# A state-space layer's chunk recurrence as a real scan after a rotation, with a new order of the stage

## The chip, the cores and the metric

The kernel runs on one core of a Trainium2 chip. The metric is the device time of one execution in microseconds (us); three runs of the kernel before gave 2777.58, 2775.36 and 2776.45 us, so a median of 2776.45.

## The reference

The model is two transformer blocks over 512 positions of width 1024. The first has two layers of a token mixer and a feed-forward part (ffn1). The second has a layer with an S5 state-space mixer and a layer with stick-breaking attention, each followed by a feed-forward part with a convolution. The change touches the S5 mixer only:

```python
u = (h @ w_in).astype(f32).reshape(bsz, seq, N_GROUPS, SSM_GROUP)
dt = jnp.exp(log_dt.astype(f32))[:, None]
mag = jnp.exp(a_re * dt)
ab_re = mag * jnp.cos(a_im * dt)
ab_im = mag * jnp.sin(a_im * dt)
...
bu_re = jnp.einsum('blgh,gph->blgp', u, bb_re)
bu_im = jnp.einsum('blgh,gph->blgp', u, bb_im)
# s[t] = ab * s[t-1] + bu[t], in complex numbers, over the sequence
_, _, s_re, s_im = lax.associative_scan(
    combine, (a_seq_re, a_seq_im, bu_re, bu_im), axis=1)
y = (jnp.einsum('blgp,ghp->blgh', s_re, c_re.astype(f32))
     - jnp.einsum('blgp,ghp->blgh', s_im, c_im.astype(f32))
     + d_skip.astype(f32) * u)
y = jax.nn.gelu(y.reshape(bsz, seq, D_SSM)).astype(h.dtype)
z = y @ w_glu
return z[..., :D_MODEL] * jax.nn.sigmoid(z[..., D_MODEL:])
```

There are 64 groups of 16 channels, and each group has 64 complex states.

## The kernel before

The sequence is cut into 64 chunks of 8 positions. Inside a chunk the work is done by matmuls with tables that are made beforehand; from chunk to chunk runs a recurrence with the factor ab to the power of 8. The channels are done in 8 tiles of 8 groups. In a tile of states one half of the 128 partitions holds the real parts and the other the imaginary parts, for 8 groups x 64 chunks. For tile i the stage has these steps, by the names that the order uses:

- `u` (four pieces, 24 matmuls): the projection w_in. VectorE takes it out of PSUM in another order of elements (`ev_u`, L1390), ScalarE's queue writes it to DRAM (`ud`), SyncE's queue reads it back with positions on the partitions (`U`).
- `S` (`states`, 8 matmuls of 64 columns, tile `vps`): what each chunk adds to the state. ScalarE copies it into `VS` (L1404).
- `c` (`scan`): the recurrence over 64 chunks, on VectorE, for parts of 2, 3 and 3 tiles: seven steps inside blocks of 8 chunks, seven from block to block, each of five operations (L1427 to L1431), a turn on ScalarE (`hs`, L1446), and for each tile three operations that make the correction `fx` (L1453 to L1455).
- `T` (`lags`, tile `yps<-U,tt`): the part of the output that comes from inside the chunk. `O` (`outs`): the part from the states, 8 matmuls on `VS` and 8 on `fx`, into the same PSUM tile.
- `G`, `H`: the gelu, Square and tanh on ScalarE and two operations on VectorE (`gq`, L1479, L1480, L1486), then a write to DRAM on ScalarE's queue (`yd`) and a read on SyncE's queue (`yT`) that turns the layout back.
- `Y` (`ysplit`): `yT` is cut into a high and a low part, `yhl`, the high one on ScalarE (L1494) and the low one on VectorE (L1495).
- `g`: tile k's share of the first four outputs of w_glu, 12 matmuls of 512 columns that read `yhl` and the split weights. The remaining w_glu outputs follow as ordinary work.

`w`, `x` and `o` load a tile's tables `wt`, `tt`, `ot` (512 KB each). A weight comes as `raw` and is split into `wh` (ScalarE, L230) and `wl` (VectorE, L233); a split is planned by a running count of TensorE's work and waits for a buffer that an earlier weight's matmuls release. The order of the stage is written out by hand in the table `ORDER`; every engine runs its instructions strictly in program order, and an instruction that issues a DMA on ScalarE's or SyncE's queue waits there as well. All tiles of 128x512 take their storage from one set of 16 slots, so a new tile waits for the last reader of the tile that had its slot.

The tables of the state-space stage are made in `ssm_gen`, as background work between the matmuls of ffn1 of the first block's second layer, from 1183 to 1425 us: `mag`, `angle`, `factor`, then `inner` and `outer` (powers of ab by doubling, `powers`, L1231 to L1237), and for each of the 8 tiles the matrices behind `ot`, `tt` and `wt`, with `go` and `gw` as tiles on VectorE and `gps` as their products on TensorE. `outer` writes `SR` and `SI`, which the scan reads.

Of the kernel before, what the change touches and what calls it, by code (L numbers as in the profile page):

```python
# [53 lines left out]
for _name, _w in (("ident", 128), ("ones_d", 128), ("ones_q", 128), ("ones_kv", 128), ("blk", 128),  # L54
# [2003 lines left out]
```

## Time and profile before

| what | before |
|---|---|
| median of three runs | 2776.45 us |
| profiled execution: its time | 2783.61 us |
| its span | 2781.9 us |
| mean granted clock of TensorE | 0.983 |
| TensorE busy | 2714.6 us (98% of the span) |
| VectorE busy | 1844.2 us (66%) |
| ScalarE busy | 1302.5 us (47%) |
| state-space stage from S0 on | 1555.33 to 1691.1 us |

TensorE is busy nearly everywhere. A busy matmul is not one at full speed: in the slices the granted clock stands at 9 tenths or more but for two slices, about 1590 to 1690 us, with 8 and 6 tenths. They are the state-space stage. "Idle before" an instruction is the time in which its engine did nothing, and the name behind the arrow is what came last before it could start.

### The profile page before, as it was taken

To read this page: it belongs to the slowest core of one execution; us is meant where nothing else is said; L and a number is where in the kernel's file an instruction comes from. 1 tells how busy PE (TensorE), PEld (TensorE's weight loads), DVE (VectorE), ACT (ScalarE), POOL (GpSimd) and SP (SyncE) were. 2 spreads that over 40 slices of the span, in tenths; PEclk is the share of its full clock that TensorE was granted. 3 is DMA by queue.
4 is the path that set the end of the run, shared out by engine and by line. 5 is a ranking of instruction groups with operands and counts; after the bars stand their busy time and mean duration, and the time that the engine had idled before them with its cause. 6 is when DMAs were issued, how large, how long until landed. Compare 5 with 4: busy or idle time off the path is not lost.

```text
span 2781.9 us, 35330 instructions
## 1 busy us (share of the span) xinstructions
PE 2714.6 (98%) x13470; PEld 2277.4 (82%) x13470; DVE 1844.2 (66%) x2963; ACT 1302.5 (47%) x2204; POOL 292.8 (11%) x311
## 2 busy tenths in 40 slices
PE   8999999999999999999999889999999999999998
PEld 6888888888878888888888788888887888888887
DVE  7889863444687997787745784555456777574544
ACT  6567553332466664533334213433235888542323
POOL 1000020000210100221002000010111111110111
PEclk9999999999999999999999868999999999999999
DMA  5323333333232334354434623333324323233321
GB/s 206 116 77 90 124 117 97 98 99 99 91 110 90 93 95 158 114 188 148 144 123 174 186 87 99 97 100 95 95 87 136 88 84 114 84 99 99 99 91 61
DMA packets 122650, 309.56 MB, mean 111 GB/s; under 512 B 35824, under 2 KB 42736, under 8 KB 122352
## 3 DMA queue, kind: packets, MB, share of 16 engines
q1 hardware_dynamic: 109424, 291.57, 32.5%
q0 software_dynamic: 2432, 7.34, 1.2%
q10 hardware_dynamic: 10624, 8.39, 1.0%
q8 instruction: 106, 1.74, 0.3%
q14 instruction: 64, 0.52, 0.1%
HBM read 260.59 MB, written 41.68 MB: 109 GB/s over the span
## 4 chain that ended last, share of the span: by engine, by line
PE 52%; DVE 5%; ACT 5%; issue 2%; POOL 1%; DMA 0%; SPq 0%; DVEq 0%; POOLq 0%; ACTq 0%
PE mm L312 46%; PE yps L312 2%; DVE wl L233 1%; PE s L312 1%; ACT e L1674 1%; PE o L312 1%; ACT e L1673 1%; ACT e L1678 1%; PE vps L312 1%; ACT wh L230 1%; DVE xg L360 0%; ACT sp L356 0%; ACT whl L356 0%; ACT w L1694 0%; PE gps L312 0%
## 5 line engine op out<-in xcount | busy, mean ns | idle before, releaser
L312 PE MATMUL mm<-xg,wh 128*128 128x512 f32 (+1 forms) x4080 | 1224.0, 382 | 26.5 <-DVE xg L360 15.7
L312 PEld LDWEIGHTS mm<-xg,wh 128*128 128x128 f32 x4080 | 747.3, 188 | 182.7 <-DVE xg L360 24.6
L230 ACT ACTIVATE wh<-raw 128x1024 fp32r<-128x1024 f32 (+2 forms) x417 | 431.0, 1039 | 826.8 <-PE mm L312 524.4
L312 PE MATMUL mm<-xg,wl 128*128 128x512 f32 (+1 forms) x2024 | 759.9, 378 | 0.0
L233 DVE TENSOR_TENSOR wl<-raw,wh 128x1024 fp32r<-128x1024 f32 (+2 forms) x417 | 528.0, 1270 | 164.7 <-ACT wh L230 159.6
L312 PE MATMUL mm<-hid,wh 128*128 128x512 f32 (+1 forms) x1816 | 539.0, 380 | 0.7 <-DVE hid L357 0.5
L312 PEld LDWEIGHTS mm<-xg,wl 128*128 128x128 f32 x2024 | 381.8, 189 | 71.3 <-issue 0.2
L312 PEld LDWEIGHTS mm<-hid,wh 128*128 128x128 f32 x1816 | 335.0, 188 | 66.8 <-DVE hid L357 1.4
L312 PE MATMUL mm<-hid,wl 128*128 128x512 f32 (+1 forms) x908 | 344.0, 379 | 0.0
L312 PE MATMUL mm<-yhl,wh 128*128 128x512 f32 x640 | 210.2, 408 | 6.9 <-DVE yhl L1495 3.7
L414 POOL TENSOR_TENSOR acc<-acc,sq 128x256 f32<-128x256 f32 (+1 forms) x90 | 106.7, 1185 | 963.7 <-ACT sq L402 875.8
L312 PEld LDWEIGHTS mm<-hid,wl 128*128 128x128 f32 x908 | 170.8, 188 | 31.9
L312 PEld LDWEIGHTS mm<-yhl,wh 128*128 128x128 f32 x640 | 122.2, 196 | 33.3 <-DVE yhl L1495 5.3
L1582 POOL TENSOR_TENSOR gt<-gt,cv 128x512 f32<-128x512 f32 x44 | 78.1, 1775 | 589.5 <-ACT wh L230 467.9
L312 PE MATMUL mm<-yhl,wl 128*128 128x512 f32 x320 | 128.6, 402 | 0.0
L591 DVE SCALAR_TENSOR_TENSOR ht<-mm,rr 128x512 f32<-128x512 f32 x64 | 43.8, 690 | 116.9 <-PE mm L312 116.6
L1590 DVE SCALAR_TENSOR_TENSOR xr<-mm,xr 128x512 f32<-128x512 f32 (+1 forms) x50 | 33.5, 670 | 124.5 <-PE mm L312 124.5
L607 DVE TENSOR_TENSOR part<-part,mm 128x512 f32<-128x512 f32 (+1 forms) x52 | 33.5, 645 | 113.9 <-PE mm L312 113.9
L1570 DVE SCALAR_TENSOR_TENSOR gt<-mm,rr 128x512 f32<-128x512 f32 x88 | 60.6, 690 | 68.1 <-PE mm L312 68.0
L722 DVE TENSOR_REDUCE nm<-s 128x1 f32<-128x512 f32 x128 | 86.7, 683 | 21.0 <-PE s L312 20.6
L749 ACT ACTIVATE pt<-pT 128x512 fp32r<-128x512 f32 x128 | 74.6, 593 | 46.3 <-PE pT L328 44.3
L729 ACT ACTIVATE p<-s,nm 128x512 f32<-128x512 f32 x128 | 87.0, 683 | 11.0 <-DVE nm L722 8.9
(295 smaller groups left out, 3461.2 us busy)
## 6 DMA issues: line engine op xcount, KB each, us to landing
raw<-in_w_up SPq DMA_DIRECT2D x152, 512.0 KB, 3.6
raw<-in_w_down SPq DMA_DIRECT2D x96, 512.0 KB, 3.5
raw<-in_w_in SPq DMA_DIRECT2D x51, 512.0 KB, 3.5
xd<-xr SPq DMA_DIRECT2D x16, 512.0 KB, 2.7
gd<-z SPq DMA_DIRECT2D x32, 256.0 KB, 2.1
g<-gd SPq DMA_DIRECT2D x32, 256.0 KB, 4.0
raw<-in_w_o SPq DMA_DIRECT2D x16, 512.0 KB, 3.6
raw<-in_w_glu SPq DMA_DIRECT2D x16, 512.0 KB, 4.2
```

The source lines that it names most:

```text
L230: ins = self.nc.scalar.activation(h, x, AF.Copy)
L233: ins = lo_engine.tensor_tensor(l, x, h.bitcast(F32), ALU.subtract)
L312: return self.nc.tensor.matmul(out, lhsT, rhs, **kw)
L414: eng.tensor_tensor(st["acc"][:, cols], st["acc"][:, cols], sq[:, cols], ALU.add)
L591: nc.vector.scalar_tensor_tensor(t, ps, 0.0, st["r"], op0=ALU.max, op1=ALU.mult)
L607: nc.vector.tensor_tensor(p, p, ps[:, cols], ALU.add)
L722: nc.vector.tensor_reduce(nm, ps, AX.X, ALU.max, negate=True)
L729: nc.scalar.activation(p, ps, AF.Exp, bias=nm, accum_out=sm)
L749: nc.scalar.activation(hi[:, :, q0:q0 + 128], v, AF.Copy)
L1570: v.scalar_tensor_tensor(t, ps, -0.5, st["r"], op0=ALU.mult, op1=ALU.mult)
L1582: nc.gpsimd.tensor_tensor(t, t, sg.pop(n), ALU.mult)
L1590: v.scalar_tensor_tensor(x, ps[:, cols], 0.5, x, op0=ALU.mult, op1=ALU.add)
```

## The change

The recurrence s[c] = a s[c-1] + v[c] has a complex factor a = m e^(i t). With z[c] = e^(-i t c) s[c] it becomes z[c] = m z[c-1] + e^(-i t c) v[c], which is real in its factor. The new stage does so for each tile by itself:

- `S` now ends with two ScalarE copies of 64x512 that swap the real and the imaginary half (`vx`).
- `b` (`load_tab`) loads a table of cos and sin for tile i (512 KB) on SyncE's queue, into one of four buffers.
- `R` (`scan`): GpSimd sets the first column of the mask `m` to zero, ScalarE fills the rest with the factor's size to the power of 8, VectorE turns v by two multiplies and an add, runs one scan instruction over 128x512 (`vz`), and ScalarE makes the negated copy with the halves swapped (`zx`, two instructions).
- `Z` (`turn`): two VectorE multiplies turn back; `O` has 8 matmuls on `vz` and 8 on `zx`, so as many as before.
- The tables come from `ssm_gen`: `turns` (the angle times 8 by three squarings), two `wheel`s in place of `outer`, and for each tile six VectorE operations of 128x512 (`table`), written to DRAM.
- `load_ops` is cut into `w` and `x`, and `ORDER` is written anew. Line numbers move with it: L312 of before is L309 now, L230 is L227, and L1404 has become L1447 and L1448.

The order's beginning, before and after (c: pieces of the old scan; R and Z of the new one):

```diff
-    u5.0 u5.1 S0 S1 u5.2 c0.0 w5 u5.3 c0.1 u6.0 c0.2 u6.1 c0.3 c0.4 w6 c0.5 c0.6 c0.7 u6.2 c0.8 w4 S2 c0.9 c0.10 w7
...
+    b0 b1 o0 u5.0 b2 u5.1 S0 R0 S1 u5.2 w4 Z0 R1 u5.3 S2 b3 Z1 S3 R2 w5 u6.0 u6.1 u6.2 Z2 R3 u6.3 T0 O0 o1 Z3 x4 S4 b4 u7.0 G0 u7.1
+    T1 O1 H0 o2 x5 R4 u7.2 G1 u7.3 Z4 w6 b5 T2 O2 H1 o3 S5 x6 w7 R5 G2 T3 O3 H2 Y0 g0 o4 Z5 S6 b6 G3 R6 T4 O4 H3 o5 x7 S7 b7 Z6 Y1 g1 G4 R7
...
+        def turns():
+
+            pr, pi = g["pr"], g["pi"]
+            m8 = self.m8 = self.apool.tile([128, 64], F32, name="m8")
+            v.tensor_tensor(m8, g["mag"], g["mag"], ALU.mult)
+            x, y = T("g_th", [64]), T("g_t", [64])
+            for k in range(3):
+                v.tensor_tensor(x, pr, pr, ALU.mult)
+                v.tensor_tensor(y, pi, pi, ALU.mult)
+                v.scalar_tensor_tensor(pi, pr, 2.0, pi, op0=ALU.mult, op1=ALU.mult)
+                v.tensor_tensor(pr, x, y, ALU.subtract)
...
+                for n in (1, 2, 4):
+                    powers(R, I, n)
+                for z, x in (("r", R), ("i", I)):
+                    t = g[name + z] = self.s2("wh" + z, F32, [128, 8, 64])
+                    nc.gpsimd.tensor_copy(t, x[:, 0:8])
+                    nc.gpsimd.tensor_copy(g["p" + z], x[:, 8])
...
+            H = lambda z: g["hi" + z][:, :, gs_].rearrange("p j g -> p g j").unsqueeze(3).to_broadcast(sh)
+            L = lambda z: g["lo" + z][:, :, gs_].rearrange("p k g -> p g k").unsqueeze(2).to_broadcast(sh)
...
+                    v.tensor_tensor(o, H("r"), L(a), ALU.mult)
+                    v.tensor_tensor(x, H("i"), L(b), ALU.mult)
+                    v.tensor_tensor(box["t"][:, k], box["t"][:, k], w, op)
+                    if k == 1:
+                        nc.sync.dma_start(self.Cd[i], box["t"])
...
         def states(i):
-            k = part[i]
...
-            self.pin(nc.scalar.copy(VS[k][:, 8 * (i - a):8 * (i - a) + 8], ps))
+            f = ps.rearrange("p g c -> p (g c)")
+            x = self.s2("vx")
+            self.pin(nc.scalar.activation(x[up], f[dn], AF.Copy))
+            self.pin(nc.scalar.activation(x[dn], f[up], AF.Copy))
+            vp[i] = f, x
+
+        def load_tab(i):
+            tab[i] = self.vpool.tile([128, 2, 512], F32, name="tab", tag="tab", bufs=4)
+            nc.sync.dma_start(tab[i], self.Cd[i])
...
+            f, x = vp.pop(i)
+            m = self.vpool.tile([128, 8, 64], F32, name="m", tag="m", bufs=2)
+            nc.gpsimd.memset(m[:, :, 0:1], 0.0)
+            self.pin(nc.scalar.activation(m[:, :, 1:64], self.m8[:, 8 * i:8 * i + 8].unsqueeze(2).to_broadcast([128, 8, 63]), AF.Copy))
+            t = self.s2("vt")
+            self.pin(v.tensor_tensor(t, f, tab[i][:, 0], ALU.mult))
+            self.pin(v.tensor_tensor(x, x, tab[i][:, 1], ALU.mult))
+            self.pin(v.tensor_tensor(t, t, x, ALU.add))
+            z = self.s2("vz")
+            self.pin(v.tensor_tensor_scan(z, m.rearrange("p g c -> p (g c)"), t, 0.0, ALU.mult, ALU.add))
+            y = self.s2("zx")
+            self.pin(nc.scalar.activation(y[up], z[dn], AF.Copy, scale=-1.0))
+            self.pin(nc.scalar.activation(y[dn], z[up], AF.Copy, scale=-1.0))
+            zs[i] = z, y
+
+        def turn(i):
+            z, y = zs[i]
+            c = tab.pop(i)
+            self.pin(v.tensor_tensor(z, z, c[:, 0], ALU.mult))
+            self.pin(v.tensor_tensor(y, y, c[:, 1], ALU.mult))
```

Three places show what moves on the engines. The first is ScalarE at the beginning of the stage. `ud2` to `ud4` are the DRAM writes of u2 to u4, the `wh` between them belongs to the weights of w_glu and waits for the matmuls of u5. Before:

```order
L230 ACTIVATE wh_14447<-raw_14248 128x1024
L1392 DMA ud2_105<-u_14377 128x8x64
L1404 COPY VS0_14466<-vps_14467 128x512
L1404 COPY VS0_14466<-vps_14477 128x512
L230 ACTIVATE wh_14515<-raw_14358 128x1024
L1392 DMA ud3_106<-u_14406 128x8x64
L1392 DMA ud4_107<-u_14442 128x8x64
L1404 COPY VS1_14604<-vps_14605 128x512
```

and now:

```order
L227 ACTIVATE wh_14597<-raw_14398 128x1024
L1436 DMA ud2_113<-u_14527 128x8x64
L227 ACTIVATE wh_14693<-raw_14508 128x1024
L1436 DMA ud3_114<-u_14556 128x8x64
L1436 DMA ud4_115<-u_14592 128x8x64
L1447 ACTIVATE vx_14633<-vps_14624 64x512
L1448 ACTIVATE vx_14633<-vps_14624 64x512
L1469 ACTIVATE m_14636<-m8_11419 128x8x63
```

The copies out of S0 and S1 (`VS0`) stood ahead of that `wh` and stand now behind it and behind both writes, as `vx`.

The second place is ScalarE between the gelus of tiles 0 to 3, ahead of the first `g` block. Before, where `yhl` is tile 0's `Y`:

```order
L1479 ACTIVATE gq_14857<-yps_14803 128x512
L332 ACTIVATE gq_14857<-gq_14857 128x512
L1487 DMA yd1_112<-gq_14857 128x512
L1494 ACTIVATE yhl_14888<-yT_14825 128x512
L1404 COPY VS2_14738<-vps_14944 128x512
L1404 COPY VS2_14738<-vps_14956 128x512
L1446 ACTIVATE hs_14975<-VS1_14604 64x168 x2
L1494 ACTIVATE yhl_15034<-yT_14879 128x512
```

and now, where `vx` to `zx` are tile 5's copies and scan neighbours, `gq_14990` is tile 2's gelu, and `yhl` is tile 0's `Y`:

```order
L1505 DMA yd1_120<-gq_14904 128x512
L1447 ACTIVATE vx_14971<-vps_14962 64x512
L1448 ACTIVATE vx_14971<-vps_14962 64x512
L1469 ACTIVATE m_14978<-m8_11419 128x8x63
L1477 ACTIVATE zx_14987<-vz_14985 64x512
L1478 ACTIVATE zx_14987<-vz_14985 64x512
L1497 ACTIVATE gq_14990<-yps_14931 128x512
L329 ACTIVATE gq_14990<-gq_14990 128x512
L1505 DMA yd2_121<-gq_14990 128x512
L1512 ACTIVATE yhl_15023<-yT_14880 128x512
L1447 ACTIVATE vx_15055<-vps_15046 64x512
L1448 ACTIVATE vx_15055<-vps_15046 64x512
```

`Y0` stood behind the write `yd1` and stands now behind `yd2`, tile 2's gelu and tile 5's part of the scan. In TensorE's order g0 comes right behind O3 now, and behind S6 and S7 before.

The third place is TensorE in the background work, at tile 0's first products (`gps`), which read `go`. Before:

```order
L312 MATMUL mm_11529<-hid_11135,wh_11286 128x512 x2
L312 MATMUL mm_11529<-hid_11135,wl_11287 128x512
L312 MATMUL gps_11567<-g_c0_11496,g_bs_11492 32x16
L312 MATMUL gps_11567<-go_11499,g_bs_11492 32x112
L312 MATMUL gps_11567<-g_c0_11496,g_bs_11492 32x16
L312 MATMUL gps_11567<-go_11499,g_bs_11492 32x112
```

and now:

```order
L309 MATMUL mm_11702<-xg_10581,wh_11536 128x512 x2
L309 MATMUL mm_11702<-xg_10581,wl_11537 128x512
L309 MATMUL mm_11702<-xg_10609,wh_11536 128x512 x2
L309 MATMUL gps_11637<-go_11575,g_bs_11568 32x112
L309 MATMUL gps_11637<-g_c0_11572,g_bs_11568 32x16
L309 MATMUL gps_11637<-go_11575,g_bs_11568 32x112
L309 MATMUL gps_11637<-g_c0_11572,g_bs_11568 32x16
L309 MATMUL gps_11637<-go_11575,g_bs_11568 32x112
```

The products that read `go` followed at once behind the first one and stand now 29 matmuls later; the first one, which reads `g_c` alone, is at its old place.

## Rows read from the trace of the kernel before

**Rows 1.** Windows of the stage: columns us, busy us of each engine, granted clock, DMA.
```profile
1588.70:1626.30 37.60, 37.60 (x167) 36.44 (x166) 35.30 (x91) 9.20 (x14) 0.00 (x0) 0.50 0.44 135
...
1646.80:1657.00 10.20, 6.39 (x14) 4.61 (x15) 9.65 (x26) 1.15 (x2) 0.00 (x0) 0.50 0.21 63
...
1663.80:1691.10 27.30, 27.02 (x104) 24.13 (x104) 9.72 (x17) 5.44 (x9) 0.00 (x0) 0.50 0.21 58
...
1555.33:1691.10 135.77, 122.46 (x643) 111.39 (x642) 101.82 (x266) 26.37 (x42) 0.00 (x0) 0.72 0.39 119
```

**Rows 2.** Timeline of TensorE in the stage: start, us, line, operation, idle before.
```profile
1559.04 1.97 PE L312 MATMUL vps<-U,wt 128*128 128x64 f32 x16 [1.54 <-issue]
...
1587.73 2.78 PE L312 MATMUL yps<-VS,ot 128*128 128x63 f32 x16 [3.12 <-DVE VS L1431]
...
1620.98 1.20 PE L312 MATMUL mm<-yhl,wh 128*128 128x512 f32 x2
...
1626.25 1.91 PE L312 MATMUL yps<-U,tt 128*128 128x64 f32 x16
...
1628.00 1.95 PE L312 MATMUL yps<-VS,ot 128*128 128x63 f32 x16
...
1648.07 2.07 PE L312 MATMUL mm<-yhl,wh 128*128 128x512 f32 x4 [2.84 <-ACT yhl L1494]
...
1661.97 2.01 PE L312 MATMUL yps<-VS,ot 128*128 128x63 f32 x16 [0.97 <-DVE VS L1431]
...
1668.89 3.64 PE L312 MATMUL yps<-VS,ot 128*128 128x63 f32 x16
...
1672.32 3.60 PE L312 MATMUL yps<-fx,ot 128*128 128x49 f32 x16
```

**Rows 3.** Groups of VectorE in the stage: busy us, mean ns, idle before.
```profile
L1431 DVE TENSOR_TENSOR VS<-VS,t 128x192 f32<-128x192 f32 x14 | 7.2, 517 | 0.4
...
L1390 DVE SCALAR_TENSOR_TENSOR u<-mm,rr 128x512 f32<-128x512 f32 x6 | 6.7, 1109 | 0.0
...
L1480 DVE SCALAR_TENSOR_TENSOR gq<-gq,yps 128x512 f32<-128x512 f32 x8 | 5.5, 686 | 16.8 <-ACT gq L1479 16.8
...
L1454 DVE TENSOR_TENSOR fx<-hs,SI 128x392 f32<-128x392 f32 x8 | 4.5, 560 | 0.1
```

**Rows 4.** The same groups for ScalarE in the stage.
```profile
L1494 ACT ACTIVATE yhl<-yT 128x512 fp32r<-128x512 f32 x8 | 4.8, 625 | 10.4 <-DVE gq L1486 6.9 <-DMA yT<-yd 3.5
...
L1404 ACT COPY VS<-vps 128x512 f32<-128x512 f32 x8 | 4.7, 585 | 33.0 <-PE vps L312 26.1 <-DVE u L1390 6.9
...
L230 ACT ACTIVATE wh<-raw 128x1024 fp32r<-128x1024 f32 x3 | 3.2, 1061 | 1.8 <-PE mm L312 1.8
```

**Rows 5.** DMA issues and their landing in us; the timeline about ud3.
```profile
ud<-u ACTq DMA_DIRECT2D x8, 256.0 KB, 4.6
U<-ud SPq DMA_DIRECT2D x8, 256.0 KB, 3.0
...
1561.46 0.38 SPq L1394 DMA_DIRECT2D U<-ud  x1
...
1563.40 1.06 ACT L230 ACTIVATE wh<-raw 128x1024 fp32r<-128x1024 f32 x1 [1.76 <-PE mm L312]
```

**Rows 6.** Windows of the background work, columns as in rows 1.
```profile
1200.00:1230.00 30.00, 30.00 (x158) 24.65 (x158) 29.97 (x83) 8.35 (x12) 14.70 (x12) 1.00 0.53 192
...
1230.00:1425.00 195.00, 195.00 (x1064) 160.53 (x1063) 134.75 (x223) 61.49 (x87) 15.01 (x28) 1.00 0.48 147
```

**Rows 7.** Timeline of all engines about tile 0's first matmuls.
```profile
1217.43 0.42 DVE L1231 TENSOR_TENSOR g_w<-gp 128x256 f32<-128x256 f32 x1
...
1218.99 3.83 POOL L1262 COPY SR<-gp 128x512 f32<-128x512 f32 x1 [6.49 <-DVE gp L1233]
...
1220.24 0.69 DVE L1284 TENSOR_TENSOR go<-go,cx 128x512 f32<-128x512 f32 x1
...
1220.63 0.36 PE L312 MATMUL gps<-go,g_bs 128*32 128x112 f32 x2
```

More of the change, by code (lines that the diff above doesn't have):

```diff
@@ new lines, in wheel, with f @@
+        def wheel(name):
+            def f():
+                R, I = [self.s4("gp", F32, [128, 16, 64]) for _ in range(2)]
+                v.memset(R[:, 0], 1.0)
+                v.memset(I[:, 0], 0.0)
+                v.tensor_copy(R[:, 1], g["pr"])
+                v.tensor_copy(I[:, 1], g["pi"])
+                for n in (1, 2, 4):
[4 more added lines that the diff above has]
+                    nc.gpsimd.tensor_copy(g["p" + z], x[:, 8])
+            return f
@@ new lines, in ssm_gen, with table, part, f @@
+        ops += [load, mag, angle, factor, inner, tables, turns, wheel("lo"), wheel("hi")]
+        def table(i):
+            box = {}
+            sh = [128, 8, 8, 8]
+            gs_ = slice(8 * i, 8 * i + 8)
+            H = lambda z: g["hi" + z][:, :, gs_].rearrange("p j g -> p g j").unsqueeze(3).to_broadcast(sh)
+            L = lambda z: g["lo" + z][:, :, gs_].rearrange("p k g -> p g k").unsqueeze(2).to_broadcast(sh)
+            def part(k, a, b, op):
+                def f():
+                    if k == 0:
+                        box["t"] = self.s4("gt", F32)
+                    o = box["t"][:, k].rearrange("p (g j k) -> p g j k", g=8, j=8)
+                    w = self.s2("cx")
+                    x = w.rearrange("p (g j k) -> p g j k", g=8, j=8)
+                    v.tensor_tensor(o, H("r"), L(a), ALU.mult)
[3 more added lines that the diff above has]
+                        nc.sync.dma_start(self.Cd[i], box["t"])
+                return f
+            return [part(0, "r", "i", ALU.subtract), part(1, "i", "r", ALU.add)]
@@ new lines, in scan @@
+        def scan(i):
+            f, x = vp.pop(i)
[12 more added lines that the diff above has]
+            zs[i] = z, y
@@ L1471, in outs @@
-            fx = FX.pop(i, None)
-            for g in range(8 if fx is not None else 0):
-                self.pin(self.mm(ps.rearrange("p g (b k) -> p g b k", b=8)[:, g, 1:8, 1:8], ot[i][:, g], fx[:, g],
-                                 start=False, stop=True, skip_group_check=True))
+            for x in zs.pop(i):
+                x = x.rearrange("p (g c) -> p g c", g=8)
+                for g in range(8):
+                    self.pin(self.mm(ps[:, g, 1:64], ot[i][:, g], x[:, g, 0:63], start=False, stop=True, skip_group_check=True))
@@ L1836, in build @@
             self.Td = [dt(f"td{i}", [128, 8, 128]) for i in range(8)]
+            self.Cd = [dt(f"cd{i}", [128, 2, 512]) for i in range(8)]
             self.wt, self.tt = {}, {}
```

100 lines of the change are left out of this document (20 added, 80 removed).

## The prediction

> **What bounds the kernel now.** I read the windows first, because the change touches one stage of some 136 us and one piece of background work. From 1555.33 us, where S0 starts, to 1691.1 us the windows give TensorE 122.46 us of work in 135.77, so 13.3 us idle, at a mean granted clock of 0.72 [rows 1]. [...] TensorE's busy time in them is 37.60 + 6.39 + 27.02 = 71.0 us; at the full level it would take half, so the lower level costs 35.5 us [rows 1], and the work itself is 122.46 - 35.5 = 87 us, say 88 since the pace of small matmuls does not quite double (16 records of a T block take 1.75 us from 1626.25, and of an O block 3.43 from 1668.89) [rows 2]. So 88 us of work, 13.3 of waits, 35 of lower clock.
>
> Then the timeline of TensorE, to see what it did before the clock fell and before it rose [rows 2]. It fell behind waits of 3.12 us (for VectorE's scan) and of 2.84 us (for ScalarE's yhl), and a third time in the small matmuls that follow a wait of only 0.97 us; a wait of 1.54 us between dense work did not lower it. It rose while the 12 matmuls of 512 columns of one `g` block ran (1620.98 to 1626.25 us: 5.27 us, or 0.22 us a matmul at the full level), and the 33 us of 64-column work ahead of that, from 1587.73 on, had not raised it. So the stage is paid for in waits of TensorE and in the clock that they take away. VectorE is the engine waited for: 101.82 us busy of 135.77, and 35.30 of 37.60 in the first slow stretch [rows 1].
>
> **What the change takes away.** The scan's VectorE work: 14 steps of five operations of 0.51 us on three tiles (35.5 us) and 24 operations of 0.56 us for `fx` (13.5) [rows 3], beside seven steps on two tiles and 21 short ones: over 50 us together. In its place each tile gets five 128x512 operations and one scan instruction. The nearest row for the five is gq (0.686 us) [rows 3]; back to back they pace about 0.6. No row shows a scan. Its bounds are 0.69 us (gq) and 1.11 us (the strided u, the dearest 512-column row) [rows 3]; I take 0.7, since its operands are contiguous as gq's are. [...] A tile costs VectorE 5 x 0.6 + 0.7 = 3.7 us, eight tiles 30 us. ScalarE gains: per tile two x copies, the mask m, two y copies, each no dearer than VS's 0.585 [rows 4], 8 x 2.9 = 23 us against 4.7 for VS. TensorE's matmuls are the same in number.
>
> So the waits for VectorE of 3.12 and 0.97 us go. What is late next is ScalarE's and VectorE's strict order and the transfers, place by place:
>
> 1. S1's wait of 1.54 us stays (its place is unchanged).
> 2. S2 and S3 now stand right behind u5, ahead of all of u6. S1 ends at 1560.8, 11 matmuls of 0.22 us bring S2 to 1563.2 [rows 2]. U2 is issued at 1561.46 and lands 3.0 us later [rows 5]: 1.2 us of wait. S3 would start at 1566.2. Its ud3 stands on ScalarE's queue behind a split wh, which before started at 1563.40 and waits for u5's end in the new order too; it takes 1.06 [rows 4, 5]. ud lands 4.6 us after its issue and U 3.0 after its own [rows 5], so U3 comes at 1571 to 1572: a wait of 5 to 6 us, and less if ud lands sooner than its median. I take 5. Before, u6's matmuls covered this.
> 3. Z2's y copies stand behind a wh that waits for the end of u7, and Z2 behind its wl: 1.06 for wh [rows 4], 1.1 for wl by the strided u and 0.69 [rows 3], 2.9 us, of which T2 covers 1.75: 1.2 us.
> 4. g0 stands right behind O3. On ScalarE the copy of tile 5 out of PSUM comes ahead of G2, and by the built program it must wait for O3's last matmul, because its tile takes a storage slot that zx of tile 3 gives back. Behind it in order: two copies (1.2), mult, mult, add and scan (2.6), two y copies (1.2), gq on both engines and tanh (0.6 + 0.69 + 0.63), the second gq (0.69), and then Y0, which waits for yd2's issue (0.6) [rows 3, 4]. That is 8.2 us with no latency in it; with some ten hand-overs 9 us. Of this chain nothing overlaps TensorE, which has no other work in its order: 9 us, the longest wait of the stage.
> 5. g1 stands behind S7 and waits for its copies and yhl: 1.2 + 0.63 [rows 4], so 2 us. g5 stands behind O7's gelu, four operations of 0.6 to 0.7 us and yhl [rows 3, 4], 3.3 us less the 2.7 of g4, with hand-overs 1.4 us.
>
> The waits are 1.5 + 1.2 + 5 + 1.2 + 9 + 2 + 1.4 = 21 us, against 13.3.
>
> Then the clock. Behind S3's wait, as behind those of 2.84 and 3.12 us, I expect the lower level until part of u6 has run: S3 1.7 us and about 15 of its 24 matmuls by 0.2 us, 5 us. At O2 the nearest row is the wait of 0.97 us in front of an O block, and there it fell [rows 2]; so O2, S5, T3 and O3 (10.5 us of full-clock work, 1.75 for eight matmuls) run at the lower level, 9.5 us dearer. The 9 us wait lowers it for g0, 2.4 us; g1 1 us. That makes 18 us, against 35.
>
> [...]
>
> Stage: 88 + 21 + 18 = 127 us for 135.8, a gain of about 9.
>
> **What it adds in the background.** The tables are built during ffn1 of the layer before, where TensorE is busy all the time and VectorE 29.97 of 30 us from 1200 to 1230 us, 134.75 of 195 after [rows 6]. `turns` (16 operations of 64 columns) and a second wheel (18 operations, the widest of them, of 256 columns, 0.42 us [rows 7], a third as many of each width) come ahead of tile 0's matmuls: some 2.5 + 4 us, and up to 3.8 us more where the second wheel waits for GpSimd's copy (a strided one took 3.83 [rows 7]; these are contiguous). Tile 0's go was finished at 1220.93, just as TensorE's first matmul on it was under way (1220.63) [rows 7]. The new order puts 29 matmuls of 0.22 us in between, 6.4 us: go is wanted at about 1227, and ready at 1220.9 plus 6.5 to 10.3, so at 1227.4 to 1231.2. A wait of 0 to 4 us for TensorE. Each tile's new table is four multiplies with one operand read at a stride and two adds: 6 x 0.69 = 4.1 us by gq, or 4 x 1.11 + 1.4 = 5.8 by u [rows 3]; 33 to 47 us in all, against 195 - 134.75 = 60 us that VectorE has free. The splits made three tiles ahead hide most. I take 2 us for go and 2 us for late splits and evacuations: 4 us, between 0 and 20 (below). The 512 KB tables go out and come back on SyncE's queue in time that DMA has; I cost them at nothing, the DMA engines being at a share of 0.48 there [rows 6], and where this cover is gone a late table costs what U3 does, some 4 us.
>
> Sum: the profiled run took 2783.6 us (span 2781.9, 1.7 around it). 2783.6 - 9 + 4 = 2778.6; the median of the runs shown, 2776.45, lies 7.2 below the profiled run, so 2771.4, say 2772 us for the median.
>
> **The rivals.**
> First, the clock holds through O2 and g1: surcharge 5 + 2.4 = 7.4, stage 88 + 21 + 8 = 117, gain 19, with 4 in the background: 2761 us. For it: 1.54 us did not lower the clock [rows 2]. Against it: 0.97 did.
> Second, slower: VectorE becomes the bound in the background. By the dear price it needs 47 + 10 of the 60 us that it has free, so nearly every burst of a table (5.8 us in one piece) makes a split or an evacuation late. It decides from about 1.1 us a multiply on. Eight tiles by 2 us and 4 for go are 20 us; with the stage at -9 that is 2776.5 + 11 = 2787 us. For it: VectorE at 29.97 of 30. Against it: the splits' lead and 7.5 us that VectorE has free for each tile.
> Third, the waits at S3 and g0 are shorter (3 and 5 us, G2 not held up) and the clock falls once: 88 + 15 + 6 = 109, gain 27, background 2: 2751 us.
> Fourth, the change doesn't do what it says: the lower clock stays through the 64-column work from S3 to g1 as it does today, and the stage keeps its 136 us: 2776 to 2782 us with the tables.
>
> **How the numbers follow.** A measurement of this kernel can't tell a change of less than about 0.2%, 5.6 us, from none: faster is under 2770.9, slower over 2782.0. Forecast 0.40 (own range 2764 to 2781; 0.14 of it faster, 0.22 same, 0.04 slower), first rival 0.20 (faster 0.18, same 0.02), second 0.20 (slower 0.18, same 0.02), third 0.08 (faster), fourth 0.12 (same 0.06, slower 0.06). Faster 0.40, same 0.32, slower 0.28. The range takes in the third rival's end and the second's dear one: 2750 to 2792.
>
> **What would show it.** In the new profile: TensorE idle ahead of g0 by 8 to 11 us, released by ScalarE's yhl; idle ahead of S3 by 3 to 7 us, released by U's transfer; VectorE in the stage at least 20 us below its 101.82 [rows 1]; the granted clock at 0.5 behind S3 and from O2 to g0; the scan between 0.69 and 1.11 us; TensorE idle for up to 4 us at about 1227 us, VectorE over 170 of 195 us behind it. If g0 follows O3 without a wait, or the clock stays up, the stage's sum is wrong on the dear side; if TensorE shows gaps through 1230 to 1425 us, the background's is wrong on the cheap side.

## The result and the profile after

The changed kernel took 2793.68 us (median of four runs, 2791.56 to 2795.40); the kernel before took 2775.9 us beside it. The ratio is 1.0067, with an interval of 1.0054 to 1.0079: slower by 17.8 us, where I had forecast 2772 us and no more than 2792. The profiled execution took 2794.77 us, its span is 2792.7.

The windows first, as in [rows 1, 6]: us, busy us of TensorE, its weight loads, VectorE, ScalarE and GpSimd, granted clock, DMA. The first one is the stage from S0 to the first matmul of the weights behind it.

```profile
1572.58:1706.58 134.00, 111.66 (x666) 101.32 (x665) 60.35 (x81) 44.34 (x69) 0.68 (x6) 0.80 0.44 136
...
1230.00:1425.00 195.00, 184.45 (x993) 151.56 (x994) 173.02 (x270) 58.16 (x82) 28.36 (x36) 0.96 0.51 158
```

The same cut of the stage in the trace of before:

```profile
1555.33:1696.04 140.71, 127.40 (x665) 115.45 (x664) 102.52 (x267) 27.36 (x43) 0.00 (x0) 0.73 0.38 114
```

S0 starts at 1572.58 us and not at 1555.33, so 17.25 us are lost before the stage begins, most of them in the stretch where TensorE had been busy for 195.00 of 195 us [rows 6] and is now for 184.45, at a granted clock of 0.96. The stage itself is 6.7 us shorter than in that execution, and VectorE's share of it has fallen by 42 us. In the stage, TensorE's waits are (start, us, line, operation, idle before and what ended it):

```profile
1583.21 3.65 PE L309 MATMUL vps<-U,wt 128*128 128x64 f32 x16 [3.78 <-DMA U<-ud]
1591.28 3.65 PE L309 MATMUL vps<-U,wt 128*128 128x64 f32 x16 [4.42 <-DMA U<-ud]
...
1620.19 1.89 PE L309 MATMUL yps<-U,tt 128*128 128x64 f32 x16
1623.29 2.00 PE L309 MATMUL yps<-vz,ot 128*128 128x63 f32 x16 [1.21 <-DVE vz L1484]
...
1627.72 3.62 PE L309 MATMUL vps<-U,wt 128*128 128x64 f32 x16
...
1651.46 1.52 PE L309 MATMUL mm<-yhl,wh 128*128 128x512 f32 x2 [9.88 <-ACT yhl L1512]
...
1667.88 1.52 PE L309 MATMUL mm<-yhl,wh 128*128 128x512 f32 x2 [1.94 <-ACT yhl L1512]
...
1699.16 1.43 PE L309 MATMUL mm<-yhl,wh 128*128 128x512 f32 x5 [1.00 <-ACT yhl L1512]
```

These are the waits that I had listed for S2, S3, O2, g0, g1 and g5, and they answer to [rows 2]; the 1.5 us that I had kept for S1 did not come. Behind the 1.21 us the pace goes from 1.9 us for 16 matmuls to 3.62: the clock fell there, as expected. At the beginning it fell a block sooner than I had it, at S2 (3.65 us).

In the background, TensorE waits at two places. The first is tile 0's `go`, the second the copy `g_bs` of tile 4's B matrix on GpSimd:

```profile
1229.01 0.61 PE L309 MATMUL mm<-xg,wh 128*128 128x512 f32 x2
1233.65 0.58 PE L309 MATMUL gps<-go,g_bs 128*32 128x112 f32 x2 [4.03 <-DVE go L1324]
...
1343.97 0.29 PE L309 MATMUL gps<-g_c,g_bs 128*32 128x16 f32 x2 [6.90 <-POOL g_bs L1358]
...
1346.54 1.22 PE L309 MATMUL mm<-xg,wh 128*128 128x512 f32 x2
```

The last row shows two matmuls of 512 columns in 1.22 us where they take 0.61 elsewhere: the lower clock comes on top of the wait. What made `g_bs` late stands on VectorE's timeline:

```profile
1337.11 0.69 DVE L588 SCALAR_TENSOR_TENSOR ht<-mm,rr 128x512 f32<-128x512 f32 x1 [3.35 <-PE mm L309]
1337.97 1.23 DVE L230 TENSOR_TENSOR wl<-raw,wh 128x1024 fp32r<-128x1024 f32 x1 [0.17 <-ACT wh L227]
1339.12 0.68 DVE L593 TENSOR_TENSOR hid<-hq,hid 128x512 fp32r<-128x512 f32 x1
1339.72 0.28 DVE L1346 TENSOR_TENSOR g_bb<-g_b,g_fr 128x128 f32<-128x128 f32 x1
```

VectorE had nothing to do for 3.35 us and then, in program order, took TensorE's last result (`ht`), a weight split and `hid` before it began tile 4's `g_bb`. TensorE's next instruction reads what comes of `g_bb`. So this is no lack of VectorE time: a piece of background work stands behind an evacuation that waits for TensorE, and TensorE waits for that piece. GpSimd's copy adds 2.63 us:

```profile
1340.94 2.63 POOL L1357 COPY g_bs<-g_bb 64x128 f32<-64x128 f32 x1 [17.10 <-DVE g_bb L1350]
1343.63 0.29 POOL L1358 COPY g_bs<-g_bb 64x128 f32<-64x128 f32 x1
```

### The profile page after: what moved, and what is told of

Read it like the earlier page. It is cut to its first block, busy times and chain, and to the rows that moved or that the text cites. A ratio compares the mean times of both kernels' runs of the same rounds, so it can differ in the third digit from the quotient of the medians.

```text
span 2792.7 us, 35332 instructions
## 1 busy us (share of the span) xinstructions
PE 2704.9 (97%) x13470; PEld 2267.8 (81%) x13470; DVE 1851.7 (66%) x2864; ACT 1320.8 (47%) x2230; POOL 301.1 (11%) x327
## 4 chain that ended last, share of the span: by engine, by line
PE 52%; DVE 5%; ACT 5%; issue 1%; DMA 1%; POOL 1%; SPq 0%; ACTq 0%; DVEq 0%; POOLq 0%
PE mm L309 46%; PE yps L309 2%; DVE wl L230 1%; PE o L309 1%; PE z L309 1%; PE s L309 1%; PE vps L309 1%; ACT e L1689 1%; PE gps L309 1%; ACT wh L227 1%; DVE xg L357 0%; ACT e L1693 0%; ACT e L1688 0%; ACT sp L353 0%; ACT whl L353 0%
## 5 line engine op out<-in xcount | busy, mean ns | idle before, releaser
L309 PE MATMUL mm<-xg,wh 128*128 128x512 f32 (+1 forms) x4080 | 1228.1, 384 | 26.0 <-DVE xg L357 14.7
L309 PEld LDWEIGHTS mm<-xg,wh 128*128 128x128 f32 x4080 | 750.8, 189 | 182.4 <-DVE xg L357 23.3
L227 ACT ACTIVATE wh<-raw 128x1024 fp32r<-128x1024 f32 (+2 forms) x417 | 431.1, 1039 | 851.9 <-PE mm L309 580.7
L309 PE MATMUL mm<-xg,wl 128*128 128x512 f32 (+1 forms) x2024 | 762.5, 379 | 0.0
L230 DVE TENSOR_TENSOR wl<-raw,wh 128x1024 fp32r<-128x1024 f32 (+2 forms) x417 | 532.5, 1281 | 187.0 <-ACT wh L227 179.4
L309 PE MATMUL mm<-hid,wh 128*128 128x512 f32 (+1 forms) x1816 | 539.3, 380 | 0.7 <-DVE hid L354 0.4
L309 PEld LDWEIGHTS mm<-xg,wl 128*128 128x128 f32 x2024 | 383.4, 189 | 72.5 <-issue 0.6
L309 PEld LDWEIGHTS mm<-hid,wh 128*128 128x128 f32 x1816 | 335.0, 188 | 67.0 <-DVE hid L354 1.4
L309 PE MATMUL mm<-hid,wl 128*128 128x512 f32 (+1 forms) x908 | 344.0, 379 | 0.0
L309 PE MATMUL mm<-yhl,wh 128*128 128x512 f32 x640 | 205.8, 401 | 12.8 <-ACT yhl L1512 12.8
L309 PEld LDWEIGHTS mm<-hid,wl 128*128 128x128 f32 x908 | 170.8, 188 | 32.1
L309 PEld LDWEIGHTS mm<-yhl,wh 128*128 128x128 f32 x640 | 119.7, 191 | 37.7 <-ACT yhl L1512 13.6
L309 PE MATMUL mm<-yhl,wl 128*128 128x512 f32 x320 | 127.0, 397 | 0.0
L726 ACT ACTIVATE p<-s,nm 128x512 f32<-128x512 f32 x128 | 87.1, 684 | 10.9 <-DVE nm L719 8.9
```

What stands on the lines that cost most here:

```text
L227: ins = self.nc.scalar.activation(h, x, AF.Copy)
L230: ins = lo_engine.tensor_tensor(l, x, h.bitcast(F32), ALU.subtract)
L309: return self.nc.tensor.matmul(out, lhsT, rhs, **kw)
L726: nc.scalar.activation(p, ps, AF.Exp, bias=nm, accum_out=sm)
```

## The experiments

The theory after this reading: the new stage is worth nothing, because the profiled execution of before ran it with a clock that was low for long, and the 17.8 us are lost in the background by the order of its pieces. Rivals: the stage gains 9 us as forecast and the background loses 27; or the six VectorE operations a table are what costs. Medians and intervals of all runs (ratios to the kernel before, run beside them on the same chip):

| run | median us | ratio | interval |
|---|---|---|---|
| before again | 2776.30 | one run | |
| new stage, old tables | 2776.92 | 1.0006 | 0.9996 to 1.0016 |
| old stage, new tables | 2802.99 | 1.0099 | 1.0084 to 1.0114 |
| no table multiplies | 2796.74 | 1.0076 | 1.0061 to 1.0091 |
| same pieces | 2787.23 | 1.0042 | 1.0030 to 1.0054 |
| Y0 early | 2786.56 | 1.0038 | 1.0027 to 1.0049 |
| same pieces, Y0 early | 2779.40 | 1.0016 | 1.0004 to 1.0027 |
| S3 behind u6 | 2794.63 | 1.0065 | 1.0048 to 1.0083 |
| wheels behind tile 0 | 2775.03 | 0.9999 | 0.9989 to 1.0009 |
| tables on GpSimd | 2792.61 | 1.0059 | 1.0039 to 1.0079 |
| spread | 2770.86 | 0.9984 | 0.9975 to 0.9993 |
| spread, gelu earlier, scan later | 2772.23 | 0.9992 | 0.9983 to 1.0001 |

**The kernel before, once more**, unchanged, for a second trace.

> The kernel before once more, for its profile. The profiled execution of before took 2783.6 us, 7 us over its timed median, with 75 us of the state-space stage at the lower clock. Theory A (the stage's gain in the two profiles, 6 us, is there only because before's profiled execution had lost its clock for longer than its timed ones do): the span is near 2775 us and the lower clock lasts some 55 to 65 us in the stage. Theory B (before always loses those 75 us): the span is 2780 to 2783 us again with the same three slow stretches.

The window of the stage, columns as above:

```profile
1556.89:1686.89 130.00, 114.91 (x665) 104.45 (x664) 102.50 (x267) 27.52 (x43) 0.00 (x0) 0.82 0.41 124
```

The same instructions took 130.00 us here and 140.71 in the trace that I had read; the granted clock is 0.82 against 0.73. How long the clock stayed low in this stage differed between these two executions of one program. The span, 2774.5 us, is 7.4 below the first one, and this stage, 10.7 us shorter, holds that difference. The two part most at one place. In the first trace an O block at 1661.97 us waits 0.97 us for `VS`, and the clock is low in the 27.30 us from 1663.80 us on [rows 1, 2]; here the last outputs of the `g` block ahead of it ran at the lower clock (0.63 us a matmul and not 0.39) and ended later, the O block did not wait, and the clock held:

```profile
1661.93 1.96 PE L312 MATMUL yps<-VS,ot 128*128 128x63 f32 x16
```

**The new stage with the old tables.** The background is left as before, and the stage reads another table of the same size in place of the cos and sin:

```diff
-            nc.sync.dma_start(tab[i], self.Cd[i])
+            nc.sync.dma_start(tab[i].rearrange("p a b -> p (a b)"), self.Td[i].rearrange("p g d -> p (g d)"))
...
-        ops += [load, mag, angle, factor, inner, tables, turns, wheel("lo"), wheel("hi")]
+        ops += [load, mag, angle, factor, inner, tables, outer]
```

> The new stage with the background work of before: no turns, no wheels, no table; the stage loads another tensor of the same size in place of the cos and sin table, so its numbers mean nothing. Theory A (the background work costs what the change lost, S0's 17 us of delay): about 2776 us, between 2770 and 2780, equal to before within a few us; TensorE waits 10 us ahead of g0 all the same. Theory B (the new stage itself is the slower one): 2785 to 2794 us.

The same window:

```profile
1556.01:1687.10 131.09, 109.26 (x666) 99.98 (x665) 60.38 (x81) 44.36 (x69) 0.67 (x6) 0.82 0.45 139
```

The stage takes 131.09 us against 130.00 for the old one, and the kernel is the same within its interval (-1.1 to +4.4 us). VectorE has 42 us less to do, TensorE is busy 5.7 us less and waits 6.7 us more (131.09 - 109.26 = 21.8 us of idle, 15.1 in the old one). The work was taken off an engine, and TensorE now waits for transfers (2.61 and 4.96 us for `U`) and for the ordered chain ahead of g0 (9.88).

**The old stage with the new tables** (`turns`, both wheels and the tables behind `outer`; nothing reads them):

```diff
-        ops += [load, mag, angle, factor, inner, tables, outer]
+        ops += [load, mag, angle, factor, inner, tables, outer, turns, wheel("lo"), wheel("hi")]
...
-                    + [spread, flip])
+                    + [spread, flip] + table(i))
```

> The stage of before with the new background work beside its own: outer stays, turns, two wheels and the eight tables are added, and nothing reads the tables. Theory A (the background work is the loss): 2792 to 2800 us, with TensorE idle ahead of tile 0's products on go for 4 us or more and once more later. Theory B (the stage is the loss): 2777 to 2784 us.

TensorE's waits from 1150 to 1480 us, by what it waited for (total us, times, longest):

```profile
PE gps L312 <- DVE go L1341: 10.8, 2, 10.0
PE gps L312 <- POOL g_bs L1375: 6.9, 1, 6.9
...
```

It is 27.6 us slower than before, so the loss lies in the background. With `outer` still there, `go` is 10 us late instead of 4. The stage itself takes 128.13 us, and the O block that waited 0.97 us in the first trace of before waits as long here, but the clock holds behind it:

```profile
1689.65 2.00 PE L312 MATMUL yps<-VS,ot 128*128 128x63 f32 x16 [0.97 <-DVE VS L1488]
```

**No table multiplies.** The tables' six operations are left out; the factors are written to DRAM in place of their products:

```diff
-                    v.tensor_tensor(o, H("r"), L(a), ALU.mult)
-                    v.tensor_tensor(x, H("i"), L(b), ALU.mult)
-                    v.tensor_tensor(box["t"][:, k], box["t"][:, k], w, op)
...
+                    nc.sync.dma_start(self.Cd[i][:, k], g["hir" if k == 0 else "hii"].rearrange("p k g -> p (k g)"))
```

> The change without the six VectorE operations of each tile's table: the two wheel tiles are written to DRAM in its place, in two transfers of 256 KB; turns and wheels stay. Theory A1 (the multiplies, 34 to 48 us of VectorE, are the loss): about 2779 us, and TensorE's wait for the copy g_bs is gone. Theory A2 (the wheels ahead of tile 0 and the shift of every background piece against TensorE's order are the loss): the wait of 4 us for go stays, one other wait for g_bs as well, 2785 to 2793 us.

The waits in the same stretch:

```profile
PE gps L309 <- POOL g_bs L1349: 8.2, 2, 6.4
PE gps L309 <- DVE go L1315: 4.0, 1, 4.0
...
```

Without 48 VectorE operations the kernel is no faster, and both waits are there. The rival that VectorE's load is the bound falls, though in the changed kernel each multiply costs 1.12 to 1.15 us.

**Same pieces.** The background is a list of pieces that is dealt out evenly between the steps of ffn1:

```python
items.extend((f, ()) for f in bg[len(bg) * i // m:len(bg) * (i + 1) // m])
```

The change makes the list 18 pieces longer (two for the wheels, two for each tile), which moves every later piece against ffn1. This run does the same work in as many pieces as before:

```diff
-        ops += [load, mag, angle, factor, inner, tables, turns, wheel("lo"), wheel("hi")]
+        ops += [load, mag, angle, factor, inner, tables, lambda: (turns(), wheel("lo")(), wheel("hi")())]
...
-                    + [spread, flip] + table(i))
+                    + [spread, flip])
...
+            g8[-1] = lambda fs=(g8[-1], *table(i)): [f() for f in fs]
```

> The change with the same instructions, but the new background work hung on to pieces that were there: turns and both wheels in one piece in outer's place, each table in the piece flip of its tile. The background list has as many pieces as before, so each piece stands where it stood against ffn1's matmuls; VectorE has as much to do as in the change. Theory P (the loss is that the 18 new pieces shift all the others, so that products on TensorE come close behind what they read): TensorE waits neither 6.9 us for g_bs nor 4 us for go, S0 near 1556 to 1560 us, 2774 to 2781 us. Theory D (the loss is VectorE's 50 us of extra work): waits of some 10 us stay, 2787 to 2795 us.

The waits again:

```profile
PE gps L309 <- DVE go L1324: 5.2, 2, 4.0
...
```

The wait for `g_bs` is gone, with the same operations on VectorE; 6.5 us of the median come back. The 4.0 us for tile 0's `go` remain, since the wheels still stand ahead of it.

**Y0 early.** Only the stage's order: tile 0's `Y0` ahead of S5 and R5, not behind H2.

```diff
-    ... H1 o3 S5 x6 w7 R5 G2 T3 O3 H2 Y0 g0 ...
+    ... H1 o3 Y0 S5 x6 w7 R5 G2 T3 O3 H2 g0 ...
```

> The change with one word of the order moved: Y0 (yhl of tile 0) ahead of S5 instead of behind H2. My account of the 9.9 us ahead of g0 (Y0 stands behind tile 5's copies, which wait for O3's end, and behind tile 2's gelu): the wait falls to 4 to 6 us (what is then left is yT0's way through DRAM or ScalarE's order), the clock rises sooner, 2778 to 2786 us. Rival (yT0 itself is late, or the order only swaps one wait for another): the wait ahead of g0 stays at 9 us or comes back at g1, 2790 to 2797 us.

TensorE's timeline at g0 and O4:

```profile
1635.55 1.52 PE L309 MATMUL mm<-yhl,wh 128*128 128x512 f32 x2 [6.37 <-ACT yhl L1512]
...
1645.99 3.65 PE L309 MATMUL yps<-vz,ot 128*128 128x63 f32 x16 [2.05 <-DMA ot<-od]
```

g0's wait falls from 9.88 to 6.37 us, and the one of 1.21 us ahead of O2 is gone, and the clock does not fall there (1.95 us a block from O2 to O3). It falls further on, at O4, which now comes sooner and waits 2.05 us for its table `ot`. The median is 7.1 us lower than the changed kernel's.

**Same pieces and Y0 early**, both edits.

> Both edits together: the background pieces as in f1_same_pieces, Y0 as in g1_y0_early. If the two losses are independent, the gains add: 2760 to 2768 us, below before's 2775.4. If the clock eats the stage's gain: 2772 to 2780 us.

A miss: 2779.40 us. The two edits did add up (6.5 + 7.1 = 13.6 us, and 14.3 were measured), but I had expected more than their sum: the wait for `go` was still to be paid, with the lower clock behind it, and O4 waits for `ot` here too (2.29 us).

**S3 behind u6.** A test of the account of S3's wait:

```diff
-    ... u5.3 S2 b3 Z1 S3 R2 w5 u6.0 u6.1 u6.2 Z2 R3 ...
+    ... u5.3 S2 b3 Z1 u6.0 u6.1 S3 R2 w5 u6.2 Z2 R3 ...
```

> The change with S3 moved behind half of u6, as S3 had cover before. My account (the waits of 3.8 and 4.4 us ahead of S2 and S3 are the price of their place): the wait ahead of S3 goes, but S3's copies and tile 3's turn come later, so TensorE waits some 5 us at O0 instead: 2790 to 2800 us, no gain. Rival (the wait at S3 is a plain loss and nothing depends on it): 2784 to 2790 us.

TensorE's waits at S3, O0 and g0:

```profile
1588.20 1.97 PE L309 MATMUL vps<-U,wt 128*128 128x64 f32 x16 [1.03 <-DMA U<-ud]
1598.29 3.67 PE L309 MATMUL yps<-vz,ot 128*128 128x63 f32 x16 [5.87 <-DVE vz L1484]
...
1649.92 1.52 PE L309 MATMUL mm<-yhl,wh 128*128 128x512 f32 x2 [15.51 <-ACT yhl L1512]
```

Covered by u6, S3 waits 1.03 us, but its scan comes later, O0 waits 5.87 and g0 15.51. No gain: S3's wait is the price of starting the chain of tile 3 early.

**Wheels behind tile 0.** Same pieces and Y0 early, with `turns` and the wheels hung on tile 0's `spread`, behind its `go`:

```diff
-        ops += [load, mag, angle, factor, inner, tables, lambda: (turns(), wheel("lo")(), wheel("hi")())]
+        ops += [load, mag, angle, factor, inner, tables, lambda: None]
...
+            if i == 0:
+                hang(-2, turns, wheel("lo"), wheel("hi"))
+            hang(-1, *table(i))
```

> As g2_same_pieces_y0_early (pieces as many as before, Y0 ahead of S5), with turns and both wheels moved out of the way of tile 0: they hang on tile 0's piece spread. If the wheels are what makes go late, the wait of 4 us at tile 0 goes and S0 comes some 5 to 8 us sooner: 2770 to 2775 us. Rival (VectorE is short of time about 1230 us whatever stands there): a wait of 2 us or more at tile 1's products instead, 2776 to 2781 us.

The waits in the background:

```profile
PE gps L309 <- DVE go L1324: 3.3, 3, 2.6
...
```

No difference from before can be measured any more. The wait at tile 0 is gone. The longest one left, 2.6 us, is for tile 1's `go`, which stands behind the clump of wheels: the sign that I had written down for the rival came as well. S0 starts at 1562.27 us, 5.4 us later than in the second trace of before, and the stage takes 5.6 us less:

```profile
1562.27:1686.65 124.38, 106.53 (x666) 96.42 (x665) 60.26 (x81) 44.36 (x70) 0.67 (x6) 0.85 0.48 146
```

**Tables on GpSimd**: the run above with `nc.gpsimd` for the six operations.

> As h2_wheels_behind_tile0, and each table's four multiplies and two adds on GpSimd instead of VectorE. GpSimd is free for most of the time from 1230 to 1425 us (15 us busy of 195 before); eight tables at about 1.8 us an operation are 85 us there. If VectorE's amount of work counts as well as its place: S0 within 2 us of before's 1555 to 1557, and with the stage of g1_y0_early (125 to 129 us for before's 130) 2768 to 2773 us, faster than before by 0.1 to 0.3%. Rival (GpSimd's strict order makes g_bs late, or GpSimd slows VectorE's operations): TensorE waits for g_bs, 2778 to 2790 us.

VectorE's groups from 1230 to 1425 us (busy us, mean ns), here:

```profile
L230 DVE TENSOR_TENSOR wl<-raw,wh 128x1024 fp32r<-128x1024 f32 x28 | 42.9, 1533 | 2.2 <-ACT wh L227 2.1
L593 DVE TENSOR_TENSOR hid<-hq,hid 128x512 fp32r<-128x512 f32 x16 | 17.0, 1062 | 1.4 <-ACT hq L592 1.3
```

and in the run before it:

```profile
L230 DVE TENSOR_TENSOR wl<-raw,wh 128x1024 fp32r<-128x1024 f32 x32 | 39.6, 1237 | 2.1 <-ACT wh L227 2.1
L593 DVE TENSOR_TENSOR hid<-hq,hid 128x512 fp32r<-128x512 f32 x16 | 11.1, 693 | 1.3 <-ACT hq L592 1.2
```

The median is 17.6 us above that run's. GpSimd ran beside VectorE, whose operations became longer, by a quarter and by a half in these two groups; `ht`, which reads one of its two inputs from PSUM, did not (685 ns here, 689 there). `go` then came late six times, 12.2 us in all.

**Spread.** `turns` and the wheels one by one on tiles 1 to 3, the tables on tiles 3 to 7, no new pieces, Y0 early:

```diff
...
+            for k, fs in {1: [(-2, [turns])], 2: [(-2, [wheel("lo")])], 3: [(-2, [wheel("hi")])]}.get(i, ()):
+                hang(k, *fs)
+            hang(-1, *[f for j in {3: [0], 4: [1], 5: [2], 6: [3, 4], 7: [5, 6, 7]}.get(i, ()) for f in table(j)])
```

> As h2_wheels_behind_tile0 (Y0 ahead of S5, no new pieces), with the new background work spread over VectorE's emptier stretches: turns with tile 1, one wheel with tile 2, the other with tile 3, and the tables from tile 3 on, the last three with tile 7. All instructions are those of the change, on the same engines. If the background's cost is where its work stands and not how much it is: no wait of TensorE for go, gw or g_bs, S0 at 1555 to 1558 us, 2766 to 2772 us. Rival (a floor of some 5 us remains, since VectorE has 47 us more to do while the splits need it): S0 at 1561 us or later, 2773 to 2780 us.

The stage and the background, columns as above:

```profile
1556.75:1677.07 120.32, 102.15 (x666) 92.18 (x665) 60.27 (x81) 44.35 (x69) 0.67 (x6) 0.89 0.49 151
1230.00:1425.00 195.00, 194.05 (x1055) 159.22 (x1054) 171.79 (x293) 60.81 (x85) 25.36 (x35) 1.00 0.49 154
```

This version is the fastest: 2770.86 us, 4.5 us under before (1.9 to 6.9 us by the interval, less than the 5.6 us that I had set as the least that can be told) and 22.8 under the changed kernel. VectorE does 171.79 us of work in the 195, as much as in the changed kernel (173.02), and TensorE loses 0.95 us instead of 10.55. S0 starts at 1556.75, and the waits of the stage are 18.2 us instead of 22.3, at a granted clock of 0.89. This trace is of a short execution, 2765.05 us, so the median says what the version is worth: the five traces with this order of the stage (the runs from "Y0 early" on, without "S3 behind u6") took 120.3 to 128.7 us for it, 124.9 in the middle, against 128.1, 130.0 and 140.7 for the old stage. O2 does not wait here, and O4, which waited 0.69 to 2.29 us for `ot` in the other four and lost the clock there, waits 0.49 and keeps it:

```profile
1606.73 1.95 PE L309 MATMUL vps<-U,wt 128*128 128x64 f32 x16
...
1630.60 2.00 PE L309 MATMUL yps<-vz,ot 128*128 128x63 f32 x16 [0.49 <-DMA ot<-od]
```

S5, T3 and O3 run at 1.95 us a block; in the changed kernel, behind the wait of 1.21 us, they took 3.62. The two halves of O2 and the four blocks of S5, T3 and O3 take 10.9 us here and took 18.3 there, so that wait cost 7.4 us of clock.

**Spread, with tile 0's gelu earlier and tile 3's scan and turn later**: R3 between T0 and O0, G0 ahead of x4, H0 ahead of u7.1, Z3 behind it.

```diff
-    ... u6.2 Z2 R3 u6.3 T0 O0 o1 Z3 x4 S4 b4 u7.0 G0 u7.1 T1 O1 H0 o2 ...
+    ... u6.2 Z2 u6.3 T0 R3 O0 o1 G0 x4 S4 b4 u7.0 H0 u7.1 Z3 T1 O1 o2 ...
```

> k6_spread with five more words of the order moved: R3 between T0 and O0, G0 ahead of x4 and H0 ahead of u7.1, so that tile 0's gelu comes ahead of tile 3's turn, and Z3 behind u7.1. If the wait of 6.4 us ahead of g0 comes from tile 0's gelu standing behind tile 3's scan: it falls to 2 us, the clock is lost once less, and the stage takes 115 to 120 us for 124: 2758 to 2765 us, faster than before by 0.4 to 0.6%. Rival (what is saved at g0 is waited for at O3 or g1): 2766 to 2772 us as k6_spread.

TensorE's waits, and the window of the stage:

```profile
1614.75 3.67 PE L307 MATMUL yps<-vz,ot 128*128 128x63 f32 x16 [1.77 <-DVE vz L1487]
1624.19 1.52 PE L307 MATMUL mm<-yhl,wh 128*128 128x512 f32 x2 [2.35 <-ACT yhl L1515]
1634.10 3.55 PE L307 MATMUL yps<-vz,ot 128*128 128x63 f32 x16 [1.70 <-DMA ot<-od]
```

```profile
1557.58:1684.67 127.09, 110.14 (x666) 99.96 (x665) 60.33 (x81) 44.35 (x69) 0.67 (x6) 0.83 0.47 143
```

g0's wait fell from 6.37 to 2.35 us. O3, which did not wait before, now waits 1.77 us for tile 3's turn, and its two halves take 3.67 and 3.62 us in place of 1.95 each: 5.2 us for the 4.0 saved. The rival, that what is saved at g0 is waited for at O3, was right. The stage took 127.09 us and not 120.32, TensorE being busy for 110.14 us at a clock of 0.83, but most of that difference is not the new order's: the medians are only 1.4 us apart, and the 1.70 us ahead of O4 are the wait for `ot` again, which the trace of the run before had at 0.49.

## Why the prediction was wrong

The trace of the changed kernel against the second one of before makes the sum: the span is 18.2 us longer, 15.7 of it before S0, 4.0 in the stage, and 1.5 less behind. My terms were +4 and -9.

**The stage, -9: the change was sized well, its base badly.** Of the waits that I listed all but S1's came, 22.3 us for my 21, a sum that is near partly by luck, since S2's is 2.6 us over and S1's 1.5 us are missing: S2 3.78 (1.2 predicted), S3 4.42 (5), O2 1.21 (1.2), g0 9.88 (9), g1 1.94 (2), g5 1.00 (1.4), with the clock falling at S2, O2, g0 and g1. O2's fall cost 7.4 us for my 9.5. Taking 9 from the 140.7 us that I read gives 131.7; the new stage took 134.0 and 131.1. But the old stage takes 130.0 in the second trace and 128.13 beside the new tables. The step that failed is the gain measured against one execution whose clock stood at 0.73: of the 35 us that I charged there to the lower clock, half of the 71.0 us that TensorE was busy in the three stretches at 0.50 of [rows 1], 12.5 are missing in the second trace, where TensorE is busy for 114.91 us in place of 127.40, and the long slow stretch from 1663.80 us on [rows 1] is missing in both other traces of the old stage. Taking off 7.2 us for the median at the end then counted the same excess twice: it came from this stage, which the change replaces.

**The background, 4 (0 to 20): mis-sized.** It is 15.7 us, of which TensorE waits 9.8 more (472.58 - 451.58 = 21.0 us from 1100 us to S0, against 456.89 - 445.69 = 11.2), and is busy 5.9 us longer for the same matmuls, at the lower clock behind those waits. The rows:

```profile
1100.00:1572.58 472.58, 451.58 (x2404) 378.57 (x2403) 355.85 (x645) 178.66 (x287) 78.54 (x85) 0.98 0.50 163
```

and of the second trace of before:

```profile
1100.00:1556.89 456.89, 445.69 (x2402) 373.93 (x2402) 309.15 (x557) 177.25 (x286) 67.00 (x75) 1.00 0.48 155
```

For `go` I took 2 of 0 to 4 us and 4.03 came. For late pieces I took 2, and one wait of 6.90 came that I had not looked for, since I counted VectorE's free time and not where each piece stands in its order. "Same pieces" shows that the length of the list made that wait. And I gave the background no price for the clock, though I had just charged the stage for it.

**The scan, 0.7 us: too cheap.**

```profile
L1475 DVE TENSOR_TENSOR_SCAN vz<-m,vt 128x512 f32<-128x512 f32 x8 | 9.8, 1225 | 1.0 <-DVE vt L1473 0.2
L1473 DVE TENSOR_TENSOR vt<-vt,vx 128x512 f32<-128x512 f32 x8 | 5.5, 690 | 0.2
```

1225 ns lies above both of my bounds, and is 1.8 times the 690 ns of an add of the same shape. The 0.7 that the sum used was my estimate from the `gq` row, and no run shows it: the scan took 1225 ns on contiguous operands. The other five operations were 0.68 to 0.69 us as taken, and ScalarE's copies 0.59 to 0.63. VectorE, busy for 60.35 of 134 us, has room for the half microsecond more; ahead of g0 the scan stands in the chain that TensorE waits for, and there it counts.

**The table multiplies, 0.69 to 1.11 us: slightly too cheap.** The second rival was to decide from 1.1 us on:

```profile
L1299 DVE TENSOR_TENSOR gt<-whr,whi 128x512 f32<-128x512 f32 x7 | 8.1, 1151 | 0.0
L1300 DVE TENSOR_TENSOR cx<-whi,whr 128x512 f32<-128x512 f32 x8 | 9.0, 1121 | 0.0
```

They are at that point, VectorE is over 170 us as I wrote, and the time, 2793.68, came nearer to that rival's 2787 than to my 2772. Its mechanism is still not the cause: leaving the operations out gains nothing, and the same operations, dealt out otherwise, cost TensorE 0.95 us.

**The first rival (the clock holds) failed at O2**: the clock fell there behind 1.21 us of idle time ahead of 64-column blocks, in all four traces that have this wait. It fell behind 1.77 us ahead of O3 as well, in the last run, while the same blocks with no wait ahead of them kept the higher level (1.95 us a block, against 3.62 behind those waits). The length of the wait does not settle it: 0.97 us ahead of the same O block were followed by the lower level in one trace of the old stage and not in another, and S1's 1.54 us, with 512-column matmuls behind the block, were not [rows 2]. The third rival asked for shorter waits than mine, and they were as long. For the stage the fourth came, no gain, but with a changed stage: less work and more waiting. The transfers of the cos and sin tables cost nothing, as taken: the eight landed 3.3 to 5.3 us after their issue, and no wait in the changed kernel names one.

Not settled: why the clock falls behind the wait of 0.97 us in one trace of the old stage and holds in another, and why the `g` block ahead of that place ran at the lower clock in the second trace of before. Of the 4.5 us of "Spread" the background has no part, S0 starting at 1556.75 us there and at 1556.89 in the second trace of before, so the traces put them in the stage; how much of them is its waits and how much that clock stays open.

## What to carry to other kernels

Before a stage is compared, read it in two executions of the same kernel: a stage whose clock moves can differ with nothing changed, here by 10.7 us, and a profile that lies 7 us above the median has its excess somewhere. Where background work is dealt out between other work, adding pieces moves all later ones: ask of each piece what stands ahead of it in its engine's order and who waits for it, since free time on the engine says nothing on that. Work taken off an engine that runs beside TensorE is worth only the waits that it ends (42 us less of VectorE's in the stage left the kernel at 1.0006), and a short wait in front of a run of small matmuls can cost several times its length in clock, here 7.4 us behind 1.21.

## What the hardware did that I had not expected

A copy on GpSimd stretched while VectorE was dense. In the changed kernel one copy of 64x128 took 9.88 us and the next 0.29:

```profile
1225.68 9.88 POOL L1357 COPY g_bs<-g_bb 64x128 f32<-64x128 f32 x1 [2.73 <-DVE g_bb L1350]
1235.61 0.29 POOL L1358 COPY g_bs<-g_bb 64x128 f32<-64x128 f32 x1
```

VectorE ran 24 two-input operations back to back through that time, busy for 9.72 of 9.72 us, and the copy ended 0.16 us after the last of them; the next copy ran while VectorE was idle. The window, columns as above:

```profile
1225.68:1235.40 9.72, 5.69 (x44) 4.62 (x43) 9.72 (x24) 1.54 (x2) 9.72 (x1) 0.90 0.42 140
```

It went the other way as well: beside GpSimd's multiplies and adds, in "Tables on GpSimd", VectorE's `wl` took 1533 ns and not 1237, and `hid` 1062 and not 693, both with two inputs in SBUF. `ht`, with one input in PSUM, kept its pace (685 and 689 ns). No run shows the cause.
